# A hybrid block on one core: the order of the delta rule's v, the attention's v, attention and z, and the pieces of the last weight loads

## The chip, the cores and the metric

The kernel runs on one core of a Trainium2 chip. The metric is the device time of one execution in microseconds, and lower is better. The kernel before takes 1188.68 us, the median of three runs (1187.45 to 1189.12).

## The reference

One block of a network on 256 tokens of width 1024, all in float32: a mixer and then a mixture of 32 experts, each with modulated RMS norms around it.

```
proj = h @ w_in                                  # 1024 -> 3592 columns
q, k, v (delta) = silu(causal_conv4(proj[:, :1536]));  z = proj[:, 1536:2048]
g, beta = gates of 4 + 4 columns
# delta rule, 4 heads of 128, chunks of 64 tokens
lower = (k*beta) @ k.T * decay * strict;  tmat = inverse(lower + eye)
u = tmat @ (v*beta);  w = tmat @ (k*beta*exp(g))
per chunk: v_new = u - w @ state;  out = q_dec @ state + attn @ v_new;  state = ...
o_a = rms_norm(out) * silu(z)
# attention, 8 heads of 64: q, k, v from the last 1536 columns, with a bias by distance
o_b = softmax(q @ k.T / 8 + bias) @ v
y = concat(o_a, o_b) @ w_out;  x = x + ga1 * rms_norm(y)
# experts: router, top 4 of 32
act = glu * sigmoid(1.702*glu) * (lin + 1)      # glu, lin = clipped halves of x @ w_up[e] + b_up[e]
out = x + ga2 * rms_norm(sum of gate * (act @ w_down[e] + b_down[e]))
```

## The kernel before, in words

The program is one sequence of instructions written in Python. A planner turns it into one queue for each engine: it knows which tiles an instruction reads and writes, gives PSUM banks out as tiles are asked for, and puts on each engine what is ready and stands first in the program. Work inside `tc.high_priority()` goes ahead of the rest. Inside `manual_schedule` (the stage after the mixer, from line 1051) TensorE and VectorE keep the order of the program.

SBUF holds ten blocks of 2 MB, "w0", "w1" and "wA" to "wH". In the mixer they hold weights, split weights and results; each has two names, as float32 (`wH_f`) and as rounded float32 (`wH_r`). Later they are the ring of the expert weights (`RINGTAGS`): each step of a group of experts loads one block for each of its experts. All loads of weights go out on SP's queue, in its order. PSUM has eight banks: three with the tag "mm", three "dl", two "tp".

**Projections.** `stream()` (line 413) goes through `halves` (line 387): for each of k, q, qb, kb (attention's q and k), vb (attention's v), v and z two halves of 256 columns. A half's weight is split by `split` into a high and a low part (ScalarE casts, VectorE and POOL subtract), and each half gives two outputs of 24 matmuls (`mm3`). The split is called two halves ahead (`sp(n + 2)`). The high part goes to one of three half blocks in turn (`highs`: both halves of wG, the first half of wH); for every third half (`n % 3 == 2`) it goes to `whx`, the second half of block H. `after` orders the later weight loads: v's into block 0 and z's into block 1. v's weight takes block 0 and vb's block D. `evac` empties a bank one step later: `conv` for k, q, v, a copy for qb, kb and vb, and `z_evac` for z.

**The delta rule.** `chain()` (line 533) is emitted after the projections up to v, with high priority. The inverse of the triangular matrices is found by doubling: the loop over `s_` from 1 to 5 (line 670) does for each level three sets of 16 small products on "dl" banks (`pair_mm`, line 638). At levels 3 and 4 it calls `ktv(a)` (line 649): four transposes of k and one scaled copy, then four transposes of v and one scaled copy into `vbt`. Behind the loop come the off-diagonal blocks (lines 703 to 711) and the heads, which use `vbt` (from line 729).

**Attention.** `attention()` (line 760) loads a strip of the relative bias (1 MB) into the second half of block H (`h2()`), masks it on POOL (line 764), and yields nine steps: scores of three groups (each on two "mm" banks, with the strip added by VectorE, line 781), transposes of the probabilities ("tp"), and products with vb. `mixed()` (line 859) puts z's four steps among attention's nine by `ZPOS`: three ahead of the first and one ahead of the third.

**Behind them.** `wout_b` multiplies attention's output with its half of `w_out` (blocks D and F), `delta_out` normalizes the delta rule's output, multiplies it with z's gate `zg` and transposes it, `wout_a` multiplies it with the other half of `w_out`, which is loaded into block 1 when z's weight is done with. Then come residual, router, gathering of tokens and the groups of experts.

**Experts.** A group of one, two or four experts has six steps, four "up" and two "down". `eload` loads a step's blocks whole, or in pieces of so many of the eight row blocks: `LAST` names the pieces for the steps of the last group, a pair.

Of the kernel before, what the change touches and what calls it, by code (L numbers as in the profile page):

```python
# [29 lines left out]
ADAPOS = [0, 2, -1, 4, 6, 8, 10, 12]  # L30
ADABANK = "tp"
KW = 2
ZPOS = [0, 2, 0, 0]

LAST = {3: (4, 4), 4: (4, 4), 5: (2, 2, 2, 1, 1)}


SINGLES, QUADS = 2, 3
# [11 lines left out]
def block_kernel(ctx, tc, x, small, rows, rel_ext, wpre, wexp, b_up, b_down, out,  # L50
# [23 lines left out]
    def bank(tag="mm"):  # L74
        return ps.tile([P, 512], F32, tag=tag, bufs=PB[tag], name=tag)
# [7 lines left out]
    def h2(dt=0):  # L83
        return fixed["wH"][dt][:, 2048:4096]
# [6 lines left out]
    def hload(i, tag, k=8):  # L91

        for h in range(2):
            nc.sync.dma_start(fixed[tag][0][:, 2048 * h:2048 * h + 2048], wpre[i][:, 2048 * h:2048 * h + 2048])
        return [[t.rearrange("p (h k n) -> p h k n", h=2, k=k)[:, h] for t in fixed[tag]] for h in range(2)]
# [18 lines left out]
    ws, sps = {}, {}  # L114
# [95 lines left out]
    def split(w, kv=None, steps=1, extra=None, copy=None):  # L210


        sr, wl = w
        kv = kv or KV
        wh = extra
        if wh is None:
            wh = highs[nsp[0] % 3]
            nsp[0] += 1
        kn = sr.shape[1]
        wh = wh.rearrange("p (k n) -> p k n", k=kn)  # L220
        st = kn // steps
        for k in range(0, kn, st):
            (copy or S.copy)(wh[:, k:k + st], sr[:, k:k + st])
            m = k + kv // steps
            V.tensor_sub(wl[:, k:m], sr[:, k:m], wh[:, k:m])
            w_ = max(1, 512 // sr.shape[2])
            for i in range(m, k + st, w_):
                G.tensor_sub(wl[:, i:i + w_], sr[:, i:i + w_], wh[:, i:i + w_])
        return wh, wl

    def mm3(b_, lhs, rhs, ks=8, late="l", first=True, last=True):


        low = (1, 0) if late == "l" else (0, 1)
        seq = [(i, j, k) for k in range(ks) for i, j in ((0, 0), (1 - low[0], 1 - low[1]))]
        seq += [(*low, k) for k in range(ks)]
        for n, (i, j, k) in enumerate(seq):
            T.matmul(b_, lhs(i, k), rhs(j, k), start=first and n == 0, stop=last and n == len(seq) - 1)  # L238
# [3 lines left out]
    vb = blC[:, 2048:3072].rearrange("p (a n) -> p a n", a=2)  # L242
# [12 lines left out]
    def hpath(j):  # L255

        c_ = slice(4 * j, 4 * j + 4)
        colvec(wsc[j], csil, adac[:, 4 * j:4 * j + 4])
        V.scalar_tensor_tensor(a1[:, c_], adac[:, c_], 1.0, sm[:, C_BADA + 8 + 4 * j:C_BADA + 12 + 4 * j],
                               op0=ALU.add, op1=ALU.add)  # L260
        V.tensor_mul(a1[:, c_], a1[:, c_], sm[:, C_NORM + 4 * j:C_NORM + 4 * j + 4])
        colvec(wsh[j], csil, adac[:, 8 + 4 * j:12 + 4 * j])
        V.tensor_add(sh1[:, c_], adac[:, 8 + 4 * j:12 + 4 * j], sm[:, C_BADA + 4 * j:C_BADA + 4 * j + 4])
        for k in range(4 * j, 4 * j + 4):
            V.tensor_scalar(xsT[:, k, :], xsT[:, k, :], a1[:, k:k + 1], sh1[:, k:k + 1], op0=ALU.mult, op1=ALU.add)
            S.copy(hh[:, k, :], xsT[:, k, :])
            V.tensor_sub(hl[:, k, :], xsT[:, k, :], hh[:, k, :])
# [79 lines left out]
    whx = h2(1)  # L347
# [36 lines left out]
        G.tensor_mul(zg[:, a, sl].rearrange("p (h d) -> p h d", h=2), zg[:, a, sl].rearrange("p (h d) -> p h d", h=2),  # L384
                     rw[:, None, R_AN:R_AN + 128].to_broadcast([P, 2, 128]))

    halves = [(nm, hf) for nm in ("k", "q", "qb", "kb", "vb", "v", "z") for hf in range(2)]

    def evac(nm, h, b_):
        if nm == "qb":  # L390
            S.mul(qbT[:, h, :], b_, 0.125)
        elif nm == "kb":
            S.copy(kbT[:, h, :], b_)
        elif nm == "vb":
            S.copy(vb[:, h % 2, 256 * (h // 2):256 * (h // 2) + 256], b_)
        elif nm == "z":
            yield from z_evac(h % 2, h // 2, b_)
        else:
            yield from conv("qkv".index(nm), h, b_)
        yield  # L400
# [3 lines left out]
    def advance():  # L404
        for g_ in list(pipe):
            if next(g_, 0) == 0:
                pipe.remove(g_)

    def flush():
        while pipe:  # L410
            advance()

    def stream():

        def sp(n):
            if n < len(halves):
                nm, hf = halves[n]
                sps[n] = split(ws[nm][hf], extra=whx if n % 3 == 2 else None)

        def after(at):  # L420
            if at == ("qb", 3):
                ws["v"] = hload(9, "w0")
            if at == ("kb", 3):
                ws["z"] = hload(10, "w1")
            if at in (("q", 3), ("v", 3), ("z", 3)):
                flush()


        sp(0)
        sp(1)  # L430
        bs = [bank(("mm", "tp")[h // 3])[:, 0:256] for h in range(4)]
        for part in range(2):
            if part:
                with tc.high_priority():
                    hpath(1)
                ws["vb"] = hload(8, "wD")
                sp(2)
            for h in range(4):
                wx, m = sps[h // 2], h % 2
                for k in range(4 * part, 4 * part + 4):  # L440
                    for n, (i, j) in enumerate(((0, 0), (1, 0), (0, 1))):
                        T.matmul(bs[h], wx[i][:, k, m * 128:(m + 1) * 128], hx[j][:, k, :],  # L442
                                 start=k + n == 0, stop=k == 7 and n == 2)
                if part:
                    if h == 2:
                        sp(3)
                    advance()
                    pipe.append(evac("k", h, bs[h]))
                    yield ("k", h)
        for n, (nm, hf) in enumerate(halves):  # L450
            if n < 2:
                continue
            sp(n + 2)
            sp_ = sps[n]
            for m in range(2):
                h = 2 * hf + m
                b_ = bank()[:, 0:256]
                if nm in ("z", "vb"):
                    mm3(b_, lambda i, k: hx[i][:, k, m * 128:(m + 1) * 128], lambda j, k: sp_[j][:, k, :], late="r")
                else:  # L460
                    mm3(b_, lambda i, k: sp_[i][:, k, m * 128:(m + 1) * 128], lambda j, k: hx[j][:, k, :])
                advance()
                pipe.append(evac(nm, h, b_))
                after((nm, h))
                yield (nm, h)
# [53 lines left out]

    bias_parts()  # L520
    st_ = stream()
    for at in st_:
        if at == ("k", 3):
# [9 lines left out]
    def chain():  # L533
# [113 lines left out]
        kdt, wT = mem.tile([P, 2, 512], F32, tag="ga2", name="kdt").rearrange("p i (h d) -> i p h d", h=4)  # L647

        def ktv(a):
            sl = slice(4 * a, 4 * a + 4)  # L650
            kp = bank("dl")
            for h in range(4):
                T.transpose(kp[:, h * 128:(h + 1) * 128], kqT[:, h, 0, a * 128:(a + 1) * 128], ident)
            V.tensor_mul((kdt, kw)[a], kp.rearrange("p (h d) -> p h d", h=4), (kd, ew)[a][:, :, None].to_broadcast([P, 4, 128]))
            vp = bank("dl")
            for h in range(4):
                T.transpose(vp[:, h * 128:(h + 1) * 128], vT[:, h, a * 128:(a + 1) * 128], ident)
            vpv = vp.rearrange("p (h d) -> p h d", h=4)
            V.tensor_mul(vbt[:, sl], vpv, betah[:, sl, None].to_broadcast([P, 4, 128]))
# [10 lines left out]
        for s_ in range(1, 6):  # L670
# [23 lines left out]
                ktv(s_ - 3)  # L694
            yield 0.6
        qd = kqT[:, :, 1, 128:256]


        def both(dst, src, scale, r_):
# [155 lines left out]
    with tc.high_priority():  # L855
        run(chain())
    wo = hload(19, "wD", 4)
    spb = [split(wo[n], kv=KW, extra=fixed["wF"][1][:, 2048 * n:2048 * n + 2048]) for n in range(2)]
    def mixed():

        att = attention(block("w0"))
        for n in range(10):
            for _ in range(ZPOS.count(n)):
                yield next(st_)
# [241 lines left out]
    def eload(regs, j, pieces=(8,)):  # L1106

        ts = [block(slot()).rearrange("p (k n) -> p k n", n=512) for _ in regs]
        k = 0
        for m in pieces:  # L1110
            for reg, t in zip(regs, ts):
                src = wexp[reg * 6 + j] if isinstance(reg, int) else wexp[bass.ds(reg * 6 + j, 1)].rearrange("o p n -> p (o n)")
                nc.sync.dma_start(t[:, k:k + m].rearrange("p k n -> p (k n)"), src[:, k * 512:(k + m) * 512])
            k += m
        return [lambda k, t=t: t[:, k, :] for t in ts]
# [180 lines left out]
    for gi, grp in enumerate(groups):  # L1296
# [7 lines left out]
        if gi + 1 < len(groups):  # L1304
            ohog = prep(groups[gi + 1])
        end_ = gi == len(groups) - 1
        cur = group(lambda j: eload(regs, j, (LAST if end_ else {5: (4, 4)} if gi == 0 else {}).get(j, (8,))),
                    cur[0], cur[1], sels, gi == 0, mid, done if end_ else None, end_)
# [101 lines left out]
```

## Time and profile before

| | |
|---|---|
| median of three runs | 1188.68 us |
| profiled execution | 1189.61 us |
| its span, first to last instruction | 1187.8 us |
| TensorE busy | 1036.5 us (87%) |
| VectorE, ScalarE, POOL busy | 315.4, 194.2, 94.4 us |
| read from HBM | 449.50 MB, 379 GB/s over the span |
| mean granted clock of TensorE | 0.948 |

All times of the trace are counted from the span's start. PE is TensorE's matmuls, PEld its weight loads, DVE VectorE, ACT ScalarE; SPq is the queue of SP. A matmul's end is modelled, so a busy TensorE is not one at its peak. In a row of the time line the bracket says how long the engine was idle before it and what ended that. "dl<-wE_f" is the tile written and one of those read; the numbers of `w0` and `w1` are left out ("w_f", "w_r").

### The profile page before, as it was taken

The numbers are of one execution on the slowest core, as the hardware profiler recorded it, in microseconds if no ns is written. First come the engines' busy times: TensorE is split into PE (matmuls) and PEld (weight loads), VectorE is DVE, ScalarE is ACT, GpSimd is POOL, SyncE is SP. The second block draws the span as 40 slices with busy tenths as digits, with TensorE's granted clock in tenths as the row PEclk, the third lists the DMA queues.
The fourth block names the chain that finished last, engine by engine and source line by source line (L and its number), as shares of the span: only waits on it lengthen the run. The fifth ranks groups of instructions, "written<-read, shape, count | busy, mean of one in ns | idle before, by whom it ended". The sixth has DMA issues, their size and how long they took to land.

```text
span 1187.8 us, 14569 instructions
## 1 busy us (share of the span) xinstructions
PE 1036.5 (87%) x5945; PEld 499.0 (42%) x5945; DVE 315.4 (27%) x802; ACT 194.2 (16%) x387; POOL 94.4 (8%) x89
## 2 busy tenths in 40 slices
PE   4899999899966799999977798999966799989986
PEld 2688888654321234434431142435421243324231
DVE  5476356454103022121211012122111011111112
ACT  3554335331000001010100001011000001010101
POOL 1546334100000000000000000000000000000000
PEclk9899999989987899999997899999987899999998
DMA  9936545769999999999999999999999999999993
GB/s 363 402 100 267 214 167 214 306 274 399 410 429 428 428 411 429 427 429 427 428 426 429 428 427 428 426 430 427 429 426 428 427 429 427 428 427 429 428 419 150
DMA packets 37348, 451.91 MB, mean 380 GB/s; under 512 B 4192, under 2 KB 5856, under 8 KB 8096
## 3 DMA queue, kind: packets, MB, share of 16 engines
q1 hardware_dynamic: 37280, 450.96, 90.8%
q8 instruction: 48, 0.79, 0.3%
q14 instruction: 20, 0.16, 0.0%
HBM read 449.50 MB, written 1.05 MB: 379 GB/s over the span
## 4 chain that ended last, share of the span: by engine, by line
PE 56%; DMA 38%; DVE 2%; ACT 2%; issue 1%; SPq 0%; POOL 0%; DVEq 0%; ACTq 0%
PE dl L1122 23%; DMA wA_f<-in_wexp_dram 11%; DMA wH_f<-in_wexp_dram 9%; PE mm L1122 9%; DMA wE_f<-in_wexp_dram 7%; PE mm L238 7%; DMA wD_f<-in_wexp_dram 6%; DMA w_f<-in_wexp_dram 3%; PE mm L1174 2%; PE tp L1011 2%; PE dl L642 2%; PE tp L203 1%; PE mm L442 1%; PE dl L238 1%; PE dl L203 1%
## 5 line engine op out<-in xcount | busy, mean ns | idle before, releaser
L1122 PE MATMUL dl<-w_f,xg 128*64 128x512 f32 (+2 forms) x224 | 108.6, 636 | 4.1 <-DMA w_f<-in_wexp_dram 4.1
L1181 DVE TENSOR_TENSOR acc<-acc,mm 128x512 f32<-128x512 f32 x50 | 34.4, 689 | 253.8 <-PE mm L1174 253.8
L1122 PE MATMUL mm<-w_f,xg 128*64 128x512 f32 (+1 forms) x208 | 92.4, 594 | 0.0
L1286 POOL TENSOR_TENSOR wC_f<-acc,m_row 128x512 f32<-128x512 f32 x2 | 2.5, 1276 | 934.0 <-DMA wA_f<-in_wexp_dram 934.0
L1140 ACT ACTIVATE sg<-gm 128x512 f32<-128x512 f32 x28 | 17.6, 630 | 298.6 <-DVE gm L1138 281.1
L1122 PE MATMUL dl<-wF_f,xg 128*64 128x512 f32 (+1 forms) x128 | 61.1, 622 | 4.0 <-DMA wF_f<-in_wexp_dram 4.0
L1122 PE MATMUL dl<-wD_f,xg 128*64 128x512 f32 (+1 forms) x128 | 60.4, 622 | 4.0 <-DMA wD_f<-in_wexp_dram 4.0
L1174 PE MATMUL mm<-yg,wts 128*128 128x512 f32 x108 | 52.6, 614 | 12.6 <-ACT yg L1172 12.6
L1122 PE MATMUL dl<-wA_f,xg 128*32 128x512 f32 (+1 forms) x96 | 51.2, 693 | 10.2 <-DMA wA_f<-in_wexp_dram 10.2
L1122 PE MATMUL dl<-wE_f,xg 128*64 128x512 f32 (+2 forms) x112 | 56.9, 662 | 3.6 <-DMA wE_f<-in_wexp_dram 3.6
L1122 PE MATMUL mm<-wB_f,xg 128*64 128x512 f32 (+2 forms) x128 | 57.2, 595 | 0.0
L1122 PE MATMUL mm<-wA_f,xg 128*64 128x512 f32 (+2 forms) x128 | 57.1, 595 | 0.0
L1122 PE MATMUL dl<-wB_f,xg 128*32 128x512 f32 (+1 forms) x96 | 52.7, 702 | 4.3 <-DMA wB_f<-in_wexp_dram 4.3
L1172 ACT COPY yg<-dl 128x512 f32<-128x512 f32 x28 | 16.4, 585 | 241.1 <-PE dl L1122 241.1
L1122 PE MATMUL dl<-wC_f,xg 128*64 128x512 f32 (+2 forms) x112 | 51.8, 610 | 3.9 <-DMA wC_f<-in_wexp_dram 3.9
L1011 PEld LDWEIGHTS tp<-oh,x 128*128 128x128 f32 x432 | 50.6, 194 | 7.6 <-issue 6.9
L1011 PE MATMUL tp<-oh,x 128*128 128x128 f32 x432 | 53.4, 280 | 0.0
L1122 PE MATMUL mm<-wE_f,xg 128*64 128x512 f32 (+1 forms) x112 | 49.8, 595 | 0.3 <-DMA wE_f<-in_wexp_dram 0.3
L1122 PEld LDWEIGHTS dl<-w_f,xg 128*64 128x64 f32 (+2 forms) x224 | 31.2, 144 | 40.5 <-issue 33.2
L1021 DVE TENSOR_SCALAR xg<-tp,mc,mc 128x128 f32<-128x128 f32 x52 | 19.6, 406 | 94.1 <-PE dl L1122 87.8
L1138 DVE TENSOR_SCALAR gm<-dl 128x512 f32<-128x512 f32 x14 | 9.7, 692 | 130.0 <-PE dl L1133 121.7
L1019 ACT ACTIVATE xg<-tp,mc,mc 128x128 f32<-128x128 f32 x52 | 21.8, 454 | 132.2 <-DVE xg L1021 132.2
(625 smaller groups left out, 2256.6 us busy)
## 6 DMA issues: line engine op xcount, KB each, us to landing
w_f<-in_wexp_dram SPq DMA_DIRECT2D x37, 2048.0 KB, 33.6
wF_f<-in_wexp_dram SPq DMA_DIRECT2D x19, 2048.0 KB, 31.6
wD_f<-in_wexp_dram SPq DMA_DIRECT2D x19, 2048.0 KB, 35.0
wE_f<-in_wexp_dram SPq DMA_DIRECT2D x19, 2048.0 KB, 36.0
wA_f<-in_wexp_dram SPq DMA_DIRECT2D x18, 2048.0 KB, 37.9
wB_f<-in_wexp_dram SPq DMA_DIRECT2D x18, 2048.0 KB, 33.6
wG_f<-in_wexp_dram SPq DMA_DIRECT2D x18, 2048.0 KB, 30.8
wC_f<-in_wexp_dram SPq DMA_DIRECT2D x18, 2048.0 KB, 32.3
```

Source lines behind the costliest of these rows:

```text
L203: T.matmul(b_[32 * i:32 * i + 32, :], vec[:, k:k + 1].to_broadcast([P, 32]), w[:, k, :], start=k < 4, stop=k >= 4)
L238: T.matmul(b_, lhs(i, k), rhs(j, k), start=first and n == 0, stop=last and n == len(seq) - 1)
L442: T.matmul(bs[h], wx[i][:, k, m * 128:(m + 1) * 128], hx[j][:, k, :], start=k + n == 0, stop=k == 7 and n == 2)
L642: T.matmul(b_[r_, c_ * 64:c_ * 64 + 64], lhs[r_, c_, :], id64[r_, :] if rhs is None else rhs[r_, c_, r_] if rhs is U else rhs[r_, c_, :], ...
L1011: T.matmul(b_[:, k * 128:(k + 1) * 128], x2[:, a, half(n)][:, k * 128:(k + 1) * 128], oh[:, a], start=a == tiles[0], stop=a == tiles[-1])
L1019: S.activation(xg[:, k], src, AF.Identity, scale=mc, bias=sc)
L1021: V.tensor_scalar(xg[:, k], src, mc, sc, op0=ALU.mult, op1=ALU.add)
L1122: T.matmul(b_[i * n:(i + 1) * n, :], lhs[:, k, i * n:(i + 1) * n], w(k), start=k == 0, stop=last and k == 7)
L1140: S.activation(sg, gm, AF.Sigmoid, scale=1.702)
L1172: S.copy(yg, b_)
L1174: T.matmul(cb, wt[:, a], yg, start=not (last and nn), stop=True)
L1181: V.tensor_add(acc[:, a, sl], acc[:, a, sl], cb)
```

## The change

The list `halves` has v ahead of vb, and their blocks are swapped accordingly: v's weight goes to block D, early, and vb's to block 0. The part of `ktv` that transposes v becomes `vtv`, called for both tiles behind the doubling loop. `ZPOS` puts z's four steps ahead of attention's third, fifth, seventh and ninth. The condition for `whx` excludes z. `LAST` gives step 2 of the last group two pieces and step 4 four.

```
-ZPOS = [0, 2, 0, 0]
-LAST = {3: (4, 4), 4: (4, 4), 5: (2, 2, 2, 1, 1)}
+ZPOS = [2, 4, 6, 8]
+LAST = {2: (4, 4), 3: (4, 4), 4: (2, 2, 2, 2), 5: (2, 2, 2, 1, 1)}
...
-    halves = [(nm, hf) for nm in ("k", "q", "qb", "kb", "vb", "v", "z") for hf in range(2)]
+    halves = [(nm, hf) for nm in ("k", "q", "qb", "kb", "v", "vb", "z") for hf in range(2)]
...
-                sps[n] = split(ws[nm][hf], extra=whx if n % 3 == 2 else None)
+                sps[n] = split(ws[nm][hf], extra=whx if n % 3 == 2 and nm != "z" else None)
...
             if at == ("qb", 3):
-                ws["v"] = hload(9, "w0")
+                ws["vb"] = hload(8, "w0")
...
-                ws["vb"] = hload(8, "wD")
+                ws["v"] = hload(9, "wD")
...
         def ktv(a):
-            sl = slice(4 * a, 4 * a + 4)
             kp = bank("dl")
             ...
             V.tensor_mul((kdt, kw)[a], kp..., (kd, ew)[a]...)
+
+        def vtv(a):
+            sl = slice(4 * a, 4 * a + 4)
             vp = bank("dl")
             for h in range(4):
                 T.transpose(vp[:, h * 128:(h + 1) * 128], vT[:, h, a * 128:(a + 1) * 128], ident)
...
                 ktv(s_ - 3)
             yield 0.6
         qd = kqT[:, :, 1, 128:256]
+        for a in range(2):
+            vtv(a)
```

## Rows read from the trace of the kernel before

**Rows 1.** Busy time by stretch (us): stretch, length, engines, granted clock, DMA share, GB/s.
```profile
131.10:221.30 90.20, 89.78 (x842) 77.71 (x841) 47.17 (x106) 41.10 (x96) 32.11 (x28) 1.00 0.54 207
...
256.60:322.40 65.80, 65.80 (x344) 26.48 (x347) 19.45 (x62) 7.93 (x14) 0.00 (x0) 1.00 0.84 340
322.40:1140.00 817.60, 708.16 (x3425) 270.80 (x3417) 142.60 (x301) 69.50 (x136) 0.00 (x0) 0.94 1.01 427
```

**Rows 2.** Chain of waits, its first long load: start, us, what.
```profile
322.44 18.88 DMA wE_f<-in_wexp_dram
```

**Rows 3.** Time line of SP's queue, the ring's second round: start, us, instruction.
```profile
265.66 0.33 SPq L1113 DMA_DIRECT2D wB_f<-in_wexp_dram  x1
```

**Rows 4.** Time line of PE, the delta rule's chain, 131 to 212 us.
```profile
131.46 1.14 PE L642 MATMUL dl<-wB_f 64*64 64x64 f32 x16
132.53 0.66 PE L653 MATMUL dl<-ident,kqT 128*128 128x128 f32 x4
...
157.94 0.27 PE L657 MATMUL dl<-ident,wB_f 128*128 128x128 f32 x1
158.14 1.15 PE L642 MATMUL dl<-wE_f,lmrow 64*64 64x64 f32 x32
...
189.85 1.14 PE L706 MATMUL dl<-wE_f 64*64 64x64 f32 x16
...
211.27 1.16 PE L756 MATMUL dl<-lmrow,wE_f 128*128 128x128 f32 x8
```

**Rows 5.** Chain of waits, pieces of TensorE's work, 122 to 212 us.
```profile
122.00 2.00 PE dl L642 x48
...
142.96 6.09 PE mm L238 x50
...
182.77 1.50 PE mm L776 x12
...
186.28 1.06 PE mm L776 x4
...
201.68 1.09 PE mm L815 x16
...
207.31 0.44 PE tp L800 x4
...
212.43 5.93 PE mm L238 x26
```

**Rows 6.** Time line of PE, z's last reads of block H.
```profile
173.07 1.20 PE L238 MATMUL mm<-wH_r,wA_r 128*128 128x256 f32 x8
```

**Rows 7.** Time line of SP's queue, the strip and the last weights.
```profile
174.35 0.39 SPq L762 DMA_DIRECT2D wH_f<-in_rel_ext_dram  x1
192.12 1.09 SPq L94 DMA_DIRECT2D w_f<-in_wpre_dram  x2
```

**Rows 8.** Time line of POOL, the strip's mask and the last weights' split.
```profile
180.51 1.49 POOL L764 TENSOR_SCALAR wH_f<-wH_f 64x512 f32<-64x512 f32 x1 [1.31 <-DMA wH_f<-in_rel_ext_dram]
...
203.22 1.29 POOL L228 TENSOR_TENSOR w_r<-w_f,wG_r 128x512 fp32r<-128x512 f32 x1
```

**Rows 9.** Time line of DVE, the first additions of the strip.
```profile
183.51 1.29 DVE L781 TENSOR_TENSOR w_f<-mm,wH_f 128x512 f32<-128x512 f32 x2
```

**Rows 10.** Busy time by stretch, after an idle gap of TensorE.
```profile
228.00:229.00 1.00, 1.00 (x3) 0.82 (x4) 0.00 (x0) 0.00 (x0) 0.00 (x0) 0.50 0.95 410
```

**Rows 11.** Time line of PE, the matmuls after that gap.
```profile
227.82 3.69 PE L238 MATMUL dl<-wH_r,wC_r 128*128 128x512 f32 x8 [2.63 <-POOL wH_f L919]
```

**Rows 12.** Time line of PE, the last group.
```profile
1139.20 0.63 PE L1150 MATMUL tp<-ident,gm 128*128 128x128 f32 x4 [1.59 <-DVE gm L1144]
```

**Rows 13.** Chain of waits, the last group.
```profile
1140.08 14.39 PE dl L1122 x64
```

**Rows 14.** Time line of SP's queue, the last group.
```profile
1150.07 0.33 SPq L1113 DMA_DIRECT2D wA_f<-in_wexp_dram  x1
```

## The prediction

> **What bounds the kernel now.** The first view to read is the busy time by stretch [rows 1]. From 322.4 us to 1140 us the transfers run at 427 GB/s with a DMA share of 1.01, and TensorE is busy 708.16 of 817.60 us: that stretch is bound by the loading of expert weights, and the chain of waits enters it at 322.44 us through a load [rows 2]. Nothing in the diff touches it except the last group. From 131.1 to 221.3 us it is the other way round: TensorE is busy 89.78 of 90.20 us, the DMA share is 0.54. The two stretches are coupled by the ring of ten weight blocks. When its first round has landed nothing can be loaded until TensorE has finished the first step of the first group; that load goes out at 265.66 us [rows 3], and from there the remaining bytes are a fixed time. So a microsecond by which TensorE reaches the experts (256.6 us) later or earlier is a microsecond at the end. The question is what the reordering does to TensorE between 131 and 257 us, and then what the smaller pieces do to the last 50 us.
>
> **The change part by part.**
>
> *Projection of v ahead of vb, v's transposes behind the doublings.* No instruction is added or removed. Before, the chain of the delta rule stalls for v: the first transposes of k end at 133.2 us, the next doubling step comes at 158.14 us, directly behind the first transpose of v at 157.94 us [rows 4]. That step does not use v. It uses two "dl" banks, and v's bank was requested ahead of them; so banks of one tag are handed out in the order of the program, and a request that cannot start holds back the later ones. With the change that stall of 25 us goes. One level takes 9.5 us where nothing stalls (from the piece at 122.00 to the one at 131.46 us) [rows 4, 5]. Levels 4 and 5 would then end near 133.3 + 2 x 9.5 = 152.3 us; from the off-diagonal product to the last product of the chain was 212.43 - 189.85 = 22.6 us [rows 4]; so the chain ends near 175 us instead of 212.4 us. The other bound is the whole stretch as it was, 212.43 - 158.14 = 54.3 us from 133.2 us on: 187.5 us. I take 175, because the 54.3 us hold further waits for v and for banks. v's conv is ready near 157 us, which the heads need at about 160 us, so its eight transposes (0.9 us) and two DVE products are beside that.
>
> By itself this is worth nothing: while the chain stalled TensorE did other work that has to be done anyway. All that moves is what is left over at the end.
>
> *Attention ahead of z.* What is left once the chain, v, vb and the column products are done is z, attention and the attention half of the output projection. From pieces of the chain of waits [rows 5]: z has 96 matmuls of 6.09/50 = 0.122 us, 11.7 us; the output half 48 of 5.93/26 = 0.228 us, 10.9 us; attention has scores of 16 x 0.125 and 16 x 0.265 us, 6.2 us, transposes of 24 x 0.11 us, 2.6 us, and products of 48 x 0.068 us, 3.3 us; eight transposes of the delta output add 0.9 us. The sum is 35.6 us, so counted back from 221.3 us the projections of v and vb end near 185.7 us, ten microseconds after the chain.
>
> There the strip of the relative bias is late. Its load (1 MB) writes the half of block H from which vb's second half is now multiplied, so it can't go out before those reads end. Before, the strip's load went out at 174.35 us, the moment z's reads of the other half of block H ended (eight from 173.07 us) [rows 6, 7]: the dependencies take block H as one piece across its two typed names. From issue to the addition on POOL took 6.16 us, that addition 1.49 us [rows 7, 8], and a DVE addition of 0.65 us frees the first score bank [rows 9]. In the changed order nothing stands between vb and the strip. vb's high half is read until eight matmuls before its end (-0.9 us), so the first bank comes free 8.3 - 0.9 = 7.4 us after vb ends. In that time TensorE has the first scores (2.0 us) and one matmul of the second (0.5 us); then all three "mm" banks are held by scores that wait for the strip. z has no bank, its first half is besides held by the write to block H, and the output half needs attention. Idle: 7.4 - 2.5 = **4.9 us**. Before, the same wait (SP sat on it) lay beside z and the chain. Bounds: nothing, if the chain has work left over; 7.4 us, if the first scores already ran among vb's matmuls. The row that it is nearest to is the strip's own, so 4.9.
>
> *Clock.* After the 2.63 us of idleness at 225 us the granted clock is 0.50 in 228 to 229 us (1.2 GHz), and eight matmuls of the output projection take 3.69 us instead of 8 x 0.228 = 1.8 us [rows 10, 11]. An idle stretch twice as long should cost that at least: **1.6 us**, bounds 0 and 3.2.
>
> *The rest of the front.* The 0.42 us of idleness between 131 and 221 us goes: **-0.4 us**. z now ends near 210 us. Then its block takes the last weights: from that issue to the last POOL subtraction of the first half of the split was 192.12 to 204.51 us, 12.4 us [rows 7, 8]; the output half left beside it (10.9 us) and the delta output's transposes cover it but for about a microsecond, and with TensorE behind anyway by the strip I cost it at nothing. hx is read until z ends, so block A's first expert load moves from 193 to about 210 us; nine loads of 2 MB at 427 GB/s (4.9 us each) from there end near 254 us, before TensorE asks for them. On SP the strip's wait holds back only the first expert loads, which aren't urgent. The condition added to the split changes nothing: z is numbers 12 and 13 of the list, and neither leaves the remainder 2.
>
> *The last group.* Step 2 in two pieces per block: TensorE stood 1.59 us until the transposes of the activations [rows 12] and then until the whole second block had landed, and then ran 14.39 us without a gap [rows 13]. With half blocks it goes on with step 2 at once (1139.20 - 1.59 = 1137.6 us) and fills that gap; but then it reaches step 3, whose last piece lands at 1150.0 us (SP issues one as one lands: 1150.07, the fourth MB after the block that ended the wait) [rows 14]. Eight pairs of 0.45 us behind that are 1153.6 us instead of 1154.5: **-0.8 us**. Bounds: 0, if the smaller transfers run slower; -1.6, if the whole gap is won. Step 4 in four pieces: TensorE never waited for it, nothing.
>
> Sum: 4.9 + 1.6 - 0.4 - 0.8 = +5.3 us on the profiled execution of 1189.61 us (span 1187.8 and 1.8 around it), 1194.9 us. That execution is 0.93 us over the median of the runs, so the forecast is **1194.0 us**.
>
> **A rule that speaks against this.** TensorE's busy share is 1.00 here, but its weight loads fill only 77.71 of the 90.20 us [rows 1]. The Trainium skill (Perfetto Trace Analysis, Identifying the Most-Contended Engine) holds matmul busy time to be no good measure of headroom and wants the busy share of LDWEIGHTS instead. By that rule up to 12.5 us of this stretch are room, and the chain which ended last could have been the bound; the rival below works it out.
>
> **The rivals.**
> - *Covered (not slower).* If the chain still has 5 us of TensorE work when vb ends, the strip's wait lies beside it. This decides from a chain end of about 190 us on; the pace with all its stalls gives 187.5. For it: DVE, ScalarE and POOL now serve the chain and the convolutions of v at once. Against it: the chain has priority, and vb, with none, is what is left. Then -0.4 - 0.8: 1187.5 us.
> - *Faster.* The chain's end was the true limit, and with it 37 us earlier TensorE packs its work closer, with the strip covered. For it: 12.5 us between weight loads. Against it: a single idle gap of 0.42 us. Between those ends I take 3 us, a quarter of the room, as every wait of another kind remains: 1188.7 - 3.0 - 0.8 = 1184.9 us.
> - *More exposed.* If z is pushed behind the output half, its weights' 12.4 us [rows 7, 8] have no cover but attention's rest: 5 us more, 1199 us. Against it: z is requested ahead of the output half.
>
> **How the numbers follow.** Forecast 0.50, covered 0.24, faster 0.20, more exposed 0.06. A measurement of this kernel can tell about 0.2%, 2.4 us, from no change. The forecast with its bounds (idle 2 to 7 us) is 1190.5 to 1197.5; a tenth of it falls within 0.2%. Slower by more than that: 0.45 + 0.06, say 0.50; within: 0.05 + 0.21, say 0.27; faster: 0.23 from the third case and the lower end of the second. The range from 1185.0 to 1198.0 us leaves out half of the faster case and the exposed one.
>
> **What would show it.** The step before v's transposes: doubling steps 9.5 us apart with no stall at 133 us, the last product of the chain before 190 us. The strip: its load issued as vb's last reads of the high half end, around 185 us, and a gap of 4 to 5 us on TensorE behind the first scores, ended by DVE's score addition, with a granted clock of 0.5 after it. The experts' first matmul near 262 us, the second round of the ring as much later. The tail: no wait before the transposes of the last group's first activations. I am wrong if TensorE has no such gap, or if a later start of the experts doesn't appear at the end.

## The result and the profile after

The changed kernel takes 1199.12 us (median of four runs, 1196.09 to 1201.26); the kernel before, on the same chip, takes 1188.42 us. The ratio is 1.009, with a 95% interval of 1.0072 to 1.0108: the change costs 10.7 us. Forecast were 1194.0 us and a range of 1185.0 to 1198.0; the measured time lies above it. The profiled execution took 1201.26 us with a span of 1199.1 us; of its lag, 1.8 us stands at 131 us already, before any matmul has moved (between 44 and 50 us the granted clock was 0.50 instead of 0.75). Line numbers behind the doubling loop are four higher than before (L1122 is now L1126).

Busy time by stretch of the kernel after; the first, third and last row answer to [rows 1].
```profile
131.10:221.30 90.20, 85.93 (x804) 75.12 (x805) 37.34 (x76) 34.72 (x85) 27.39 (x24) 0.96 0.40 146
190.00:205.00 15.00, 10.73 (x60) 9.03 (x62) 5.50 (x12) 6.39 (x27) 4.57 (x4) 0.77 0.25 70
271.30:335.10 63.80, 63.80 (x344) 25.97 (x347) 19.50 (x62) 7.94 (x14) 0.00 (x0) 1.00 0.91 367
335.10:1140.00 804.90, 695.92 (x3365) 260.79 (x3359) 139.92 (x297) 68.89 (x134) 0.00 (x0) 0.94 1.01 427
```
TensorE, which lacked 0.42 us of the first stretch before, now lacks 4.27 us. The experts' stretches begin later. The first, with the same 344 matmuls, is 2.0 us shorter (63.80 against 65.80 us).

Time line of SP's queue after: the strip, the last weights [rows 7], the ring's second round [rows 3].
```profile
189.41 0.39 SPq L766 DMA_DIRECT2D wH_f<-in_rel_ext_dram  x1
...
219.50 0.82 SPq L94 DMA_DIRECT2D w_f<-in_wpre_dram  x2
...
278.81 0.33 SPq L1117 DMA_DIRECT2D wB_f<-in_wexp_dram  x1
```
The strip's load goes out 15.1 us later than before, the last weights 27.4 us, the ring's second round 13.15 us.

Time line of PE after, 134 to 272 us; the first three rows answer to [rows 4], the later ones to [rows 11], the last is the experts' first matmul.
```profile
134.34 0.66 PE L652 MATMUL dl<-ident,kqT 128*128 128x128 f32 x4
134.93 1.14 PE L642 MATMUL dl<-wE_f,lmrow 64*64 64x64 f32 x16
...
190.47 1.16 PE L760 MATMUL dl<-lmrow,wE_f 128*128 128x128 f32 x8
191.56 1.57 PE L780 MATMUL mm<-wC_f 64*128 64x128 f32 x12
197.40 2.07 PE L780 MATMUL mm<-wC_f 64*128 64x256 f32 x4 [4.27 <-DVE w_f L785]
199.40 3.78 PE L238 MATMUL mm<-wH_r,wA_r 128*128 128x256 f32 x16
...
206.46 2.16 PE L238 MATMUL mm<-wH_r,wA_r 128*128 128x256 f32 x16
...
226.09 1.98 PE L238 MATMUL mm<-wF_r,wC_r 128*128 128x512 f32 x8
...
239.15 3.78 PE L238 MATMUL mm<-wF_r,wC_r 128*128 128x512 f32 x8 [3.21 <-ACT wH_f L842]
242.73 1.91 PE L238 MATMUL mm<-wD_r,wC_r 128*128 128x512 f32 x4
...
251.97 2.06 PE L238 MATMUL mm<-wH_r,wC_r 128*128 128x512 f32 x8 [1.60 <-DVE wH_f L926]
...
271.28 0.64 PE L1126 MATMUL mm<-wB_f,xg 128*64 128x512 f32 x1
```
The doublings no longer stall: the next level stands right behind k's transposes. The bracket at 197.40 us is the strip's wait; z's first 16 matmuls behind it take 3.78 us, the same 16 at 206.46 us take 2.16. The bracket at 239.15 us is new, and the eight matmuls behind it take 3.78 us, where the same form took 1.98 at 226.09 us. What it waits for is seen on ScalarE and POOL.

Time lines after of ACT (first row) and, in the second fence, of POOL.
```profile
238.51 1.07 ACT L842 COPY wH_f<-mm 128x512 f32<-128x512 f32 x2 [1.95 <-POOL w_r L228]
```
```profile
228.63 2.62 POOL L228 TENSOR_TENSOR w_r<-w_f,wG_r 128x512 fp32r<-128x512 f32 x2 [7.52 <-DVE w_r L225]
235.88 2.60 POOL L228 TENSOR_TENSOR w_r<-w_f,wH_r 128x512 fp32r<-128x512 f32 x2 [4.62 <-DVE w_r L225]
```
The copy empties the banks of attention's output half into `yb`, which is the second half of block H. The split of the last weights keeps the high part of its second half in the first half of block H, and POOL reads it until 238.5 us. The two halves hold different data, but the dependency goes by the whole block; so both banks of the output half stay full until the split is over. I call this the wait in block H. Before, the split ended near 210.5 us, and the same copies ran at 210.51 and 215.44 us. Time lines before of POOL and, in the second fence, of ACT:
```profile
207.85 2.62 POOL L228 TENSOR_TENSOR w_r<-w_f,wH_r 128x512 fp32r<-128x512 f32 x2 [3.34 <-PE tp L800]
```
```profile
210.51 0.59 ACT L838 COPY wH_f<-mm 128x512 f32<-128x512 f32 x1 [0.22 <-DVE rso0x L145]
...
215.44 0.59 ACT L838 COPY wH_f<-mm 128x512 f32<-128x512 f32 x1 [1.08 <-PE mm L238]
```

Chain of waits after, the last group (to [rows 12, 13]).
```profile
1044.58 39.90 DMA wA_f<-in_wexp_dram
...
1151.74 4.29 PE dl L1126 x18
...
1156.61 14.32 PE dl L1126 x62
```
From 1084.5 us on no load stands in the chain. The experts' first matmul came 14.7 us later than before (271.28 against 256.59 us). The ring's second round came 13.15 us later, as it goes out 7.53 us behind that matmul and not 9.07. The last instruction came 11.3 us later. So the time from the second round to the end is 1.85 us shorter, in one execution of each kernel; how much of that the last group's pieces give is tried below.

### The profile page after: what moved, and what is told of

It reads as the page before. It is cut to its first block, busy times and chain, and to the rows that moved or that the text cites. A ratio compares the mean times of both kernels' runs of the same rounds, so it can differ in the third digit from the quotient of the medians.

```text
span 1199.1 us, 14596 instructions
## 1 busy us (share of the span) xinstructions
PE 1043.3 (87%) x5945; PEld 499.5 (42%) x5945; DVE 315.0 (26%) x802; ACT 194.7 (16%) x387; POOL 94.8 (8%) x89
## 4 chain that ended last, share of the span: by engine, by line
PE 67%; DMA 26%; DVE 3%; ACT 2%; issue 1%; POOL 0%; SPq 0%; ACTq 0%; DVEq 0%; POOLq 0%
PE dl L1126 28%; PE mm L1126 13%; DMA wA_f<-in_wexp_dram 11%; PE mm L238 7%; DMA wH_f<-in_wexp_dram 6%; DMA wE_f<-in_wexp_dram 4%; PE tp L1015 3%; PE mm L1178 3%; DMA wD_f<-in_wexp_dram 3%; PE dl L642 2%; DMA w_f<-in_wpre_dram 2%; PE tp L203 1%; PE mm L442 1%; PE tp L1154 1%; PE dl L203 1%
## 5 line engine op out<-in xcount | busy, mean ns | idle before, releaser
L1126 PE MATMUL dl<-w_f,xg 128*64 128x512 f32 (+2 forms) x224 | 105.7, 623 | 3.5 <-DMA w_f<-in_wexp_dram 3.5
L1126 PE MATMUL mm<-w_f,xg 128*64 128x512 f32 (+1 forms) x208 | 92.2, 593 | 0.0
L1126 PE MATMUL dl<-wF_f,xg 128*64 128x512 f32 (+1 forms) x128 | 63.3, 638 | 3.9 <-DMA wF_f<-in_wexp_dram 3.9
L1126 PE MATMUL dl<-wD_f,xg 128*64 128x512 f32 (+1 forms) x128 | 61.7, 630 | 3.8 <-DMA wD_f<-in_wexp_dram 3.8
L1126 PE MATMUL mm<-wA_f,xg 128*64 128x512 f32 (+2 forms) x128 | 57.1, 595 | 1.2 <-DMA wA_f<-in_wexp_dram 1.2
L1126 PE MATMUL dl<-wE_f,xg 128*64 128x512 f32 (+2 forms) x112 | 53.5, 630 | 4.9 <-DMA wE_f<-in_wexp_dram 4.9
L1126 PE MATMUL mm<-wB_f,xg 128*64 128x512 f32 (+2 forms) x128 | 57.4, 595 | 0.0
L1126 PE MATMUL dl<-wA_f,xg 128*32 128x512 f32 (+1 forms) x96 | 49.2, 670 | 9.1 <-DMA wA_f<-in_wexp_dram 9.1
L1126 PE MATMUL dl<-wC_f,xg 128*64 128x512 f32 (+2 forms) x112 | 53.0, 624 | 3.8 <-DMA wC_f<-in_wexp_dram 3.8
L1126 PE MATMUL dl<-wB_f,xg 128*32 128x512 f32 (+1 forms) x96 | 50.7, 680 | 3.0 <-DMA wB_f<-in_wexp_dram 3.0
L1126 PE MATMUL mm<-wE_f,xg 128*64 128x512 f32 (+1 forms) x112 | 49.9, 594 | 0.0
L1126 PEld LDWEIGHTS dl<-w_f,xg 128*64 128x64 f32 (+2 forms) x224 | 30.5, 141 | 35.6 <-issue 29.0
```

Of the source, the lines that this page charges most:

```text
L1126: T.matmul(b_[i * n:(i + 1) * n, :], lhs[:, k, i * n:(i + 1) * n], w(k), start=k == 0, stop=last and k == 7)
```

## The experiments

All were timed beside the kernel before, which took 1188.5 to 1188.9 us; ratios are to it. None leaves work out.

**The parts of the change.** Theory at first: attention ahead of z is all of the loss, v's move is worth nothing.

*z put back*: the changed kernel with
```
-ZPOS = [2, 4, 6, 8]
+ZPOS = [0, 2, 0, 0]
```


> The changed kernel with z put back ahead of attention (ZPOS as before); v ahead of vb, v's transposes behind the doublings and the smaller last pieces stay. Theory (all of the loss comes from attention ahead of z, that is from the strip's exposed load and from the late last weights; v's move is worth nothing): 1187 us, between 1185.5 and 1188.5, the part under 1188.4 being the last group's 0.8 to 1.8 us; the experts' first matmul at 256 to 258 us. Rival (v's move or the later transposes cost too): 1192 us or more, with the experts' first matmul behind 261 us.


1201.24 us, 1.0101 [1.0084, 1.0118]. The theory fell: without attention ahead of z the change costs as much. *That part alone* in the kernel before:


> The kernel before with attention ahead of z alone (ZPOS as in the change). Theory: slower by most of what the change lost, 1194 to 1199 us: the last weights again wait for z's end near 219 us, while the strip's load may be partly covered, since the chain still ends late here. Rival (the change's parts cost only together, since the early end of the chain is what exposes the strip): 1189 us or less.


1195.57 us, 1.0049 [1.0031, 1.0067]; as the theory has it. The strip's load goes out at 162.85 us, and the wait behind the first scores is 0.60 us. *The pieces of the last group alone*:


> The kernel before with the smaller pieces of the last group alone (LAST as in the change). Theory: 0.8 to 1.8 us faster, 1186.6 to 1187.6 us; no wait ahead of the transposes of the last group's first activations (1.59 us before). Rival (smaller transfers run slower, the last piece lands later): 1188.4 us or above.


1188.01 us, 0.999 [0.998, 1.0]: 0.9 us, at the edge of what can be measured.

*v's transposes behind the doublings, alone* (the kernel before with `vtv` as in the change):


> The kernel before with v's transposes put behind the doublings and nothing else of the change. Theory of now (the chain's late end was the cover: with the doublings no longer held by v the chain ends near 191 us instead of 212, its matmuls stand ahead of the last projection, and the strip's load and the softmax steps have nothing beside them): 1196 to 1201 us, last projection's end near 190 us, chain's last product near 190 us. Rival (the order of v and vb makes the strip late, since vb's second half is then what is read from block H last): 1191 us or less.


1201.12 us, 1.0093 [1.0071, 1.0116]: the reordering that was worth nothing costs 12.5 us. That is just above the range of the theory, and its chain's end was wrong: the last product is at 206.2 us, not near 190. What moved is the strip's load, from 174.35 to 187.44 us, and behind it TensorE waits for attention's steps (first two rows). The third row is the wait of 2.63 us in [rows 11], a little longer. Time line of PE of this run:
```profile
212.03 0.63 PE L804 MATMUL tp<-ident,w_f 128*128 128x128 f32 x4 [2.19 <-ACT w_f L805]
...
214.71 1.98 PE L819 MATMUL mm<-w_f,wC_f 128*64 128x128 f32 x16 [2.05 <-DVE wC_r L825]
...
240.66 3.24 PE L238 MATMUL dl<-wH_r,wC_r 128*128 128x512 f32 x8 [2.99 <-POOL wH_f L923]
```
*The same part taken back* from the changed kernel:


> The changed kernel with v's transposes put back in front of the last doublings; the order of v and vb, attention ahead of z and the last pieces stay. Theory of now (the early end of the chain exposes the strip): strip covered, chain's last product behind 200 us; the late last weights stay, so 1193 to 1196 us, like attention ahead of z alone. Rival (the order of v and vb exposes it): 1198 us or more, with a gap of 3 us or more behind the first scores.


1189.24 us, 0.9997 [0.9982, 1.0012]: 9.9 us better than the change, with attention still ahead of z. The time is below the range of the theory, and the chain's last product ends at 196.85 us, not behind 200; but the strip is covered, as the theory has it: its load goes out at 177.43 us, and TensorE does not wait for it. Busy time of PE on "dl" banks, up to the end of vb's projection and behind it, first fence of this run, second of the change:
```profile
131.00:178.20 47.20, 14.24 (x240) 1.00 0.52 201
178.20:200.00 21.80, 9.41 (x80) 1.00 0.42 146
```
```profile
131.00:189.90 58.90, 25.05 (x313) 1.00 0.54 203
189.90:200.00 10.10, 1.16 (x8) 0.87 0.37 105
```
In the change 10.8 us more of the chain stand ahead of vb's end, and vb ends 11.7 us later (0.8 of it is a later start of that execution). Taken back, those matmuls stand beside the strip's load.

**The two waits.** *The wait in block H taken away* (from here on the cure of block H): the high parts of both halves of the split in block G.
```
-    spa = [split(wo[n], kv=KW) for n in range(2)]
+    spa = [split(wo[n], kv=KW, extra=highs[1 - n]) for n in range(2)]
```


> The changed kernel, with the high parts of both halves of the last weights' split put into block G, so that the write of attention's first output half into block H no longer waits for the reads of the split. Theory (half of the loss is this wait: the second set of the output product starts at 244.4 us instead of about 239): 1194 us, between 1192 and 1196, and no gap of 3.2 us on TensorE ended by ScalarE's write into block H. Rival (only the strip matters, this gap is filled by another wait, the weights themselves being late): 1198 us or more.


1189.63 us, 1.0011 [1.0002, 1.0021]: 9.5 us, about twice what was expected. The copies now wait for TensorE. Time line of ACT of this run:
```profile
224.19 0.59 ACT L842 COPY wH_f<-mm 128x512 f32<-128x512 f32 x1 [0.82 <-PE mm L238]
229.69 0.59 ACT L842 COPY wH_f<-mm 128x512 f32<-128x512 f32 x1 [2.68 <-PE mm L238]
```
*The strip's wait taken away*: the high parts of vb's and z's second halves go to block G, and the split of vb's is called one half ahead instead of two.
```
+                own = {11: highs[0], 13: highs[1]}.get(n, whx if n % 3 == 2 else None)
+                sps[n] = split(ws[nm][hf], extra=own)
```


> The changed kernel; the high parts of vb's second half and of z's second half are split into the working blocks of the split instead of block H, so the strip of the relative bias no longer waits for vb's end. Theory (the strip's wait is a cost of its own): the idle 4.3 us behind the first scores and the half clock after them (about 2 us) go, 1191 to 1195 us. Rival (the time is handed on, since the last weights and the output's write into block H end the front anyway): 1197 us or more.


1190.53 us, 1.0014 [1.0001, 1.0027]: 8.6 us. The load goes out at 149.73 us, the gap behind the scores is gone, the other wait stays. Time line of PE of this run:
```profile
228.84 3.04 PE L238 MATMUL mm<-wF_r,wC_r 128*128 128x512 f32 x8 [3.22 <-ACT wH_f L846]
```
*Both*:


> The changed kernel with both cures: the strip no longer waits for vb, and the output no longer waits in block H for the split of the last weights. Theory (the change's two waits are separate places and everything it lost is in them): 1182 to 1186 us, at or near the kernel before with the second cure alone (1184.7). Rival (each cure took the same time, 8.5 and 9.5 of 10.5 us lost, since one wait lies in the other's shadow): 1188 us or more.


1181.55 us, 0.9943 [0.9926, 0.9959]. The costs add up: 8.1 us for the strip (from 1189.63), 9.0 for block H (from 1190.53), 17.6 together.

*The cure of block H in the kernel before*, and *with the last group's pieces too*:


> The kernel before with the high parts of both halves of the last weights' split in block G. Theory (the write of the output into block H waits for reads of the split here too): TensorE's waits of 2.63 us at 225 us and 1.60 us at 235 us go, with the half clock behind the first (1.6 us): 1183 to 1186 us. Rival (these waits are the normalisation's own latency and come back in another place): 1188 us or more.


1184.72 us, 0.9963 [0.995, 0.9976]. So the same wait cost 3.9 us in the kernel before.


> The kernel before with the smaller last pieces and with the high parts of the last weights' split in block G. Theory: the two gains add up, 1183 to 1184.5 us. Rival (the last group's gain is within the spread): 1184.7 us or above.


1181.10 us, 0.9934 [0.9917, 0.995]. This is the changed kernel's time with both cures, to half a microsecond: apart from the two waits the change as a whole moves nothing. Its parts do, as the last runs show. *Attention ahead of z alone, with the cure of block H*:


> The kernel before with attention ahead of z alone (1195.6 us), and with the high parts of the last weights' split in block G. Theory (attention ahead of z costs through the output's write into block H alone, which waits for the later split): 1184 to 1187 us, as the kernel before with the same cure (1184.7). Rival (the later loading itself costs): 1191 us or more.


1186.37 us, 0.999 [0.9976, 1.0005]; without the cure it was 1195.57. Of the 6.6 us of that part 1.7 are left (1186.37 - 1184.72).

**Is it the two waits everywhere?** *Levels 4 and 5 and all behind them without priority*, in the changed kernel:
```
+    ch = chain()
     with tc.high_priority():
-        run(chain())
+        for _ in range(12):
+            next(ch)
+    run(ch)
```


> The changed kernel, but the last two doubling levels and all that follows in the chain have no priority and stand behind vb's projection in the program; nothing else is put back. Theory of now (v's transposes used to hold the doublings back; without them their 12.8 us of matmuls stand ahead of the projections, which moves the strip's load by that much and leaves that much less work to lie beside it): vb ends near 177 us, the strip's load goes out by 178 us, no gap of over 1 us behind the first scores, 1187 to 1191 us. Rival (what costs is that v's transposes come late, so that the heads and the chain's end are late): 1198 us or more.


1194.29 us, 1.0036 [1.0011, 1.0062], with runs from 1186.8 to 1198.2 us: between the two expectations, and inconclusive in size. The strip's load goes out at 162.16 us and no gap stands behind the first scores, but a short new gap is followed by a low clock (last section).

*v ahead of vb* in the kernel before with the last pieces and the cure of block H (1181.10 us without it):


> As the run before this one, and v's projection ahead of vb's, with v's transposes and z left where they were. Theory (v's projection by itself moves nothing but what waits for v: the chain's last product comes before 200 us, the strip's load with vb's end near 177 us, still beside work): 1182 to 1185 us. Rival (v ahead of vb costs by itself): 1187 us or more.


1195.83 us, 1.0055 [1.0038, 1.0071]: the rival held, at a cost of 14.7 us. The strip's load goes out at 188.13 us, and then attention's steps stand alone. Time line of PE of this run:
```profile
199.00 1.13 PE L776 MATMUL mm<-wC_f 64*128 64x256 f32 x4 [1.10 <-DVE w_f L781]
...
208.37 0.43 PE L815 MATMUL mm<-w_f,wC_f 128*64 128x128 f32 x2 [1.58 <-ACT w_f L801]
...
214.18 1.12 PE L800 MATMUL tp<-ident,w_f 128*128 128x128 f32 x4 [3.11 <-POOL w_f L789]
...
218.64 2.40 PE L815 MATMUL mm<-w_f,wC_f 128*64 128x128 f32 x18 [1.07 <-DVE wC_r L821]
```
*That kernel, and the one with v's later transposes alone, with the strip's load freed* (the high parts of v's or vb's second half and of z in block G):


> The kernel with v ahead of vb, the smaller last pieces and the split in block G (1195.8 us), with the strip's load freed in the same way. Theory (the order of v and vb costs through the strip's load alone, issued at 188 us there): 1181 to 1185 us. Rival: 1192 us or more.


1191.25 us, 1.0022 [1.0012, 1.0032].


> The kernel before with v's transposes behind the doublings alone (that run took 1201.1 us), and with the high parts of v's second half and of both halves of z split into block G, so that nothing that the strip's load waits for in block H is read after the first half of v. Theory (v's later transposes cost through the strip's load alone, which they push from 174 to 187 us): 1188 to 1192 us, the strip's load out before 170 us. Rival (they cost by the order of the matmuls itself): 1197 us or more.


1196.77 us, 1.0071 [1.0053, 1.0089]. Each gains 4.4 to 4.6 us, so both come out between the theory and its rival, near the rival, and 8 to 10 us stay: there is a third wait. With z ahead of attention and the chain's work early, nothing lies beside the softmax steps. Time line of PE of the second of these runs, whose profiled execution was its fastest (1193.47 us; bracket: DVE's part of the evacuation of attention's product), and its busy time:
```profile
211.19 0.43 PE L821 MATMUL mm<-w_f,wC_f 128*64 128x128 f32 x2 [3.21 <-DVE wC_r L827]
```
```profile
205.00:222.00 17.00, 13.40 (x96) 10.03 (x96) 12.77 (x31) 11.51 (x27) 7.04 (x6) 0.90 0.46 181
```
The same stretch of the kernel before and, in the second fence, of the change with both cures:
```profile
205.00:222.00 17.00, 17.00 (x114) 14.57 (x112) 9.83 (x37) 9.07 (x27) 2.54 (x2) 1.00 0.61 222
```
```profile
205.00:222.00 17.00, 17.00 (x113) 14.31 (x113) 10.51 (x37) 9.00 (x25) 4.03 (x4) 1.00 0.69 278
```
TensorE's idle time from 205 to 222 us (17.00 us less its busy time), by what stands behind or beside attention:

| kernel | idle, us |
|---|---|
| before (z ahead, chain late) | 0.00 |
| change, and change with both cures (z among attention's steps) | 0.00 |
| z put back; v's transposes late; v ahead of vb (z ahead, chain or projection early) | 5.31; 4.24; 6.07 |
| the last two with the strip freed | 3.60; 3.86 |

The idleness is not the whole of the 8 to 10 us; the granted clock is below 1.00 in these stretches too (0.90 and 0.71 in the last two), and no run takes this wait away by itself. Two kernels not in the table, the change with the strip freed and the one with v's transposes taken back, have 1.35 us there, ahead of the delta output's transposes.

*Without the late transposes, with the cure of block H, the rest as changed*:


> The changed kernel with v's transposes put back in front of the last doublings (1189.2 us) and with the high parts of the last weights' split in block G. Theory (the strip is covered here, at 177 us, and the one wait left is the one in block H, 7 to 9 us): 1180 to 1183 us. Rival (half of that wait is the normalisation's own): 1185 us or more.


1177.92 us, 0.9914 [0.9894, 0.9933]: below both expectations, and the fastest kernel here, 11.0 us under the kernel before. The strip's load goes out at 174.47 us, TensorE is busy 17.00 of 17.00 us in that stretch, and the experts' first matmul comes at 248.0 us. Its busy time in the first stretch of [rows 1]:
```profile
131.10:221.30 90.20, 90.20 (x835) 77.73 (x834) 49.45 (x107) 41.78 (x97) 30.72 (x27) 1.00 0.51 195
```
It is also 3.2 us under the kernel before with the same cure and last pieces (1181.10). So v ahead of vb, which costs 14.7 us with z ahead of attention, gains together with attention ahead of z; where these 3.2 us come from was not taken apart.

## Why the prediction was half right

*What bounds the kernel.* Right in the main: the experts' first matmul came 14.7 us later and the end 11.3; 1.5 us were won back in the first step and 1.85 behind the second round.

Two steps failed: that v's move is worth nothing by itself, and that z's late weights cost nothing.

*v ahead of vb, transposes later: nothing by itself.* This step failed. The reason given, that TensorE did other work while the chain stalled, is true and is why it costs: the stalled chain was the work that lay beside the strip's load and attention's steps. Alone it costs 12.5 us, within the change 9.9. The prediction did count what is left at the end, and found the strip uncovered, but charged it to attention ahead of z; in the run with the transposes taken back attention stays ahead of z and the strip is covered, and with attention ahead of z alone only 0.60 us of its wait show.

*The strip: 4.9 us of idleness and 1.6 us of clock.* The mechanism was right. Idle were 4.27 us. The half clock cost 3.1 us: 0.9 in the four scores behind the gap (2.07 us, against 1.13 for the same form in the run with v ahead of vb), and 2.1 in the 24 matmuls of z behind them (3.78 + 1.64 against 2.16 + 1.12). That is 7.4 us for 6.5 forecast, with the clock at about twice its term and inside its bounds. Freeing the load gains 8.1 to 8.6. The load was forecast near 185 us; it went out at 189.4, 1.8 of it the late start of this execution.

*z's late weights at nothing.* This term made the error in size. The cure of block H gains 9.5 us in the change and 3.9 in the kernel before, so 5.6 us came with the change (2.1 by the runs with the other cures: 9.0 against 1188.01 - 1181.10 = 6.9). Three things in the step were wrong. z ended at 219.4 us, not near 210, as its matmuls were spread through all of attention. The output half was to cover the load and split; three of its four sets of matmuls did, but the fourth had no bank (239.15 us), since the first is emptied into block H behind that split. And [rows 11] were read as the price of a gap, where asking what the gap in the old order waited for would have led to `yb`. The dependency across the two names of block H had been seen for the strip, and was not asked of block H's next user. The rival "more exposed" gave 1199 us, with a chance of 0.06, and it had the late weights right; but its condition did not hold, since z ended at 219.4 us, ahead of the output half, and not behind it. That its time is the measured one is luck.

*Sum.* Strip 8.1, block H 2.1 to 5.6, last group -0.9: 9.3 to 12.8 us, for 10.7 measured and 5.3 forecast.

*The last group: -0.8 us.* Alone 0.9, with an interval that reaches up to no change (1.0). The wait of 1.59 us before the last group's transposes is gone in the changed kernel, as forecast.

*The chain near 175 us, at most 187.5.* It ended at 191.6. Level 4 took 12.5 us (134.93 to 147.43 us), not 9.5, though no stall for v was left. That makes "covered" and "faster" wrong as well: at 191.6 us the chain was past the 190 us from which "covered" was to decide, yet only eight of its matmuls were left behind vb.

*Weight loads as headroom.* In the stretch from 131 us, weight loads fill 75.12 of 90.20 us, less than before, and the time rose. The Trainium skill (Perfetto Trace Analysis, Identifying the Most-Contended Engine) judges TensorE's headroom by the busy share of weight loads, together with the share of peak arithmetic (MFU). No run here shows TensorE using that room: in the fastest kernel weight loads fill 77.73 us of this stretch, as before (77.71), and it gained by filling gaps.

## What to carry to other kernels

A chain that ends last may be the cover of everything beside it. Before a stall on a busy engine is taken away, list what that engine does meanwhile and which transfers and latencies then lie beside the moved work. Ending the stall is worth nothing if the order that it frees only empties another place. When one wait is found to go by a whole block, follow that block to its next writer and reader: the same false dependency can hold them too, as it held the output half here.

## What was not expected of the hardware

A short gap can be followed by a loss in clock that is longer than the gap, and the length of the gap alone does not decide it. In the run with the late levels a gap of 1.10 us (time line of PE, first fence) is followed by ten microseconds at a granted clock of 0.50, 1.2 GHz (busy time by stretch, second fence):
```profile
179.19 1.68 PE L642 MATMUL dl<-wE_f,lmrow 64*64 64x64 f32 x16 [1.10 <-DVE wB_f L686]
```
```profile
175.00:180.00 5.00, 3.90 (x45) 3.40 (x44) 4.57 (x9) 3.55 (x17) 2.65 (x3) 0.96 0.00 0
180.00:185.00 5.00, 5.00 (x25) 3.12 (x23) 1.28 (x3) 2.68 (x8) 4.54 (x5) 0.50 0.02 3
185.00:190.00 5.00, 5.00 (x54) 4.69 (x53) 4.54 (x9) 2.07 (x8) 0.00 (x0) 0.50 0.00 2
```
In the change the clock was at 0.50 for about six microseconds behind the longer gap of 4.27 us (first row), and at 1.00 behind the gap of 1.60 us that ends at 251.97 us (second and third row). Busy time by stretch:
```profile
198.00:204.00 6.00, 6.00 (x25) 5.26 (x24) 3.99 (x9) 4.83 (x23) 2.39 (x3) 0.50 0.00 0
252.00:254.00 2.00, 2.00 (x9) 1.68 (x10) 1.90 (x7) 0.27 (x1) 0.00 (x0) 1.00 1.01 434
254.00:258.00 4.00, 4.00 (x45) 3.58 (x43) 1.49 (x7) 2.72 (x8) 0.00 (x0) 1.00 1.01 434
```
What tells these gaps apart was not tried. That the spread of the runs with the late levels (11 us) comes from whether the clock falls there is a guess; only one execution of it was profiled.
